# Bias by distance of four heads in one matmul of four rows, the rows repeated by the DMA that writes them

## The chip, the cores and the metric

One core of a Trainium2 chip runs the whole program. The metric is device time in microseconds (us), the median of several executions. The core has TensorE (matmuls, PE in the profile; PEld are its weight loads), VectorE (DVE), ScalarE (ACT), GpSimd (POOL) and SyncE (SP), which here issues nearly all DMA transfers, and sixteen DMA engines that carry them out.

## The reference

A decode step of a hybrid layer. One branch is a gated linear recurrence; the other, where the change lies, is attention in a sliding window with a dilation: three groups of four heads, window 128, 512 or 2048, dilation 1, 4 or 16. A score gets a bias that depends only on the head and on the distance of key and query:

```
def slot_bias(rel_bias, g):
    dist = jnp.arange(N_SLOTS, dtype=jnp.int32) * DILATIONS[g]
    return rel_bias[t5_bucket(dist), g * HEADS_PER_GROUP:(g + 1) * HEADS_PER_GROUP].astype(jnp.float32)
...
    dist = qi + BLK - ki
    in_band = (dist >= 0) & (dist <= N_BACK)
...
    b = jnp.transpose(bias[jnp.clip(dist, 0, N_BACK)], (2, 0, 1))
    s = jnp.einsum('brnqhe,brnkhe->brnhqk', qc, kb, preferred_element_type=jnp.float32)
    s = s * ATTN_SCALE + b
```

## The kernel before

The order of all instructions is written out by hand, and each engine takes its own in that order. The first thousand microseconds are a loop over `units` (index `i`): twelve heads in the order of groups 2, 1, 0, and for each head 16 blocks of 128 tokens and a unit for the 64 sample tokens, so 17 units (`ph = i % 17`) to a head. A unit makes q, k and v of its block (`stage_a`, 24 matmuls z<-w,RH or z<-w,RL on L336, about 5 us), normalizes and transposes them (trc, L376), makes scores S and adds the bias tile T3 (L401, L407), takes the exponential, and multiplies with v; stages of up to four units are interleaved.

The bias of a head is a table of 383 values, one for each distance and BIG where the window ends. `bias_0` loads a 33 x 383 onehot matrix `oh` (L281) and spreads the head's column of `reln` over 128 columns (`lb`, L283). `bias_a` multiplies the two (L290), so that 128 equal rows of 383 come out, copies them to `es_` (L292) and writes them to device memory, to `Dsc[hd]` (L293). `bias_b` reads them back with a row step of 382 in place of 383 (L298, L299), which shifts each row by one against the row ahead of it: that is `T3`, the bias of a block of queries against a block of keys. `bias_0` of the next head `nh` stands at unit 7 of a head, `bias_a` at unit 9, `bias_b` at unit 12. For the first head all stand at the start.

At the start and again while the last head of group 2 and of group 1 runs (`i // 17` 3 and 7), the units also bring in the input x: `x_load` (xt, 512 KB, L224, two buffers), `x_mul` on VectorE (L240, two halves), `x_tr` (transposes trx and the split into RH and RL). At the start `x_norm` takes the squares on ScalarE first (L229). A tile loaded in one unit is used in the next. Other transfers of these stretches are kv outputs (L371), attention outputs Osc (L435), weights wr (L307) and copies from cache to cache out_kv_s (L109), all issued by SyncE in one sequence; an issue waits until what it reads is made and its buffer is free.

Of the kernel before, what the change touches and what calls it, by code (L numbers as in the profile page):

```python
# [11 lines left out]
F32 = mybir.dt.float32  # L12
# [11 lines left out]
HD = 128  # L24
# [6 lines left out]
NBX = 383  # L31
# [11 lines left out]
def program(tc, I, O, C, upto=99, debug=False):  # L43
    nc = tc.nc
    es = ExitStack()
    G = K()
# [4 lines left out]
    PE, ACT, DVE, POOL = nc.tensor, nc.scalar, nc.vector, nc.gpsimd  # L51
    dma = nc.sync.dma_start
# [6 lines left out]
    Dsc = sd("Dsc", [12, 128, NBX])  # L59
# [18 lines left out]
    def pool(stack, name, **kw):  # L78
        return stack.enter_context(tc.tile_pool(name=name, bufs=1, reuse_waits="tile", **kw))
# [5 lines left out]
    ps = es.enter_context(tc.tile_pool(name="ps", bufs=2, space=PSUM))  # L85
# [108 lines left out]
    ap_ = pool(at, "ap")  # L194
    xs_ = ExitStack()
    reln = ap_.tile([33, 12], F32, name="reln")
# [78 lines left out]
    heads = [(g, h) for g in (2, 1, 0) for h in range(4)]  # L275
    Wt, Wr, Tt = {}, {}, {}

    def bias_0(g, h):
        hd = g * 4 + h
        oh = ap_.tile([128, NBX], F32, name="oh", tag="wraw", bufs=4)  # L280
        dma(oh[0:33, :], C["onehot"][:, g, :])  # L281
        lb = ap_.tile([128, HD], F32, name="lb", tag="kqs", bufs=1)
        POOL.tensor_copy(lb[0:33, :], reln[:, hd:hd + 1].to_broadcast([33, 128]))  # L283
        G.ohlb = oh, lb

    def bias_a(g, h):
        hd = g * 4 + h
        oh, lb = G.ohlb
        eb = ps.tile([128, NBX], F32, name="eb", tag="op")
        PE.matmul(eb, lb[0:33, :], oh[0:33, :], start=True, stop=True)  # L290
        es_ = ap_.tile([128, NBX], F32, name="es_", tag="wraw", bufs=4)
        ACT.copy(es_, eb)  # L292
        dma(Dsc[hd], es_)  # L293

    def bias_b(g, h):
        hd = g * 4 + h
# [13 lines left out]
    def w_conv_h(hd_, k):  # L310
        w = ap_.tile([128, 2, 384], F32R, name="w", tag="w", bufs=10)
        ACT.copy(w[:, 0, :], Wr[hd_, k])
        Wt[hd_, k] = w
# [5 lines left out]
    def w_conv(hd_, k, eng):  # L319
        wr = Wr.pop((hd_, k))  # L320
        w = ap_.tile([128, 2, 384], F32R, name="w", tag="w", bufs=10)
        split(w[:, 0, :], w[:, 1, :], wr, eng)
        Wt[hd_, k] = w
# [14 lines left out]
    def stage_b1(u):  # L338
        m, z = u.m, u.z
        if u.stacked:  # L340
            DVE.tensor_add(z[0:NS], z[0:NS], u.zl[0:NS])
        u.ss = ap_.tile([128, 2], F32, name="ss", tag="ss", bufs=3)
        jk = ap_.tile([128, HD], mybir.dt.bfloat16, name="jk", tag="jk", bufs=1)
        for i in range(2):
            ACT.activation(jk[0:m, :], z[0:m, i * 128:(i + 1) * 128], AF.Square, accum_out=u.ss[0:m, i:i + 1])  # L345
        u.rs = ap_.tile([128, 2], F32, name="rs", tag="rs", bufs=3)
        POOL.tensor_scalar(u.ss[0:m, :], u.ss[0:m, :], 1.0 / HD, EPS, ALU.mult, ALU.add)  # L347
        POOL.tensor_tensor(u.rs[0:m, :], u.ss[0:m, :], neghalf[0:m, :], ALU.pow)  # L348

    def stage_b2h(u):  # L350
        m, z = u.m, u.z
        u.vt = ap_.tile([128, 2, HD], F32R, name="vt", tag="vt", bufs=4)
        return u.vt[0:m, 0, :], z[0:m, 256:384]
# [19 lines left out]
    def stage_c(u):  # L373
        m = u.m
        tr = ps.tile([128, 2, 128], F32, name="trc", tag="tr")
        PE.transpose(tr[:, 0, 0:m], u.kvo[0:m, 0, :], ident[0:m, 0:m])  # L376
        PE.transpose(tr[:, 1, 0:m], u.qn[0:m, :], ident[0:m, 0:m])
        if u.smp:
            u.kq = ap_.tile([128, 2, NS], F32, name="kqs", tag="kqs", bufs=1)
            ACT.copy(u.kq, tr[:, :, 0:m])  # L380
        else:
            split(KQ[:, u.slot, :, 0, :], KQ[:, u.slot, :, 1, :], tr, DVE)
# [116 lines left out]
    x_mul(1, D // 2, D)  # L499
    POOL.tensor_scalar(gq, gq, -SCALE, 0.0, ALU.mult, ALU.add)  # L500
    POOL.tensor_scalar(reln[0:32, :], reln[0:32, :], -1.0, 0.0, ALU.mult, ALU.add)
    bias_0(*heads[0])
    w_conv(heads[0], 6, DVE)
    w_conv(heads[0], 7, DVE)
    N = len(units)
# [2 lines left out]
    kqs = []  # L508
# [27 lines left out]
    for i in range(N + 3):  # L536
        u, u1, u2, u3 = get(i), get(i - 1), get(i - 2), get(i - 3)
        nh = heads[i // 17 + 1] if i // 17 + 1 < len(heads) and u is not None else None
        ph = i % 17
        G.i = i  # L540
        late = u1 and u1.stacked
        if late:
            u1.zl = ap_.tile([128, 384], F32, name="zl", tag="wraw", bufs=4)
            ACT.copy(u1.zl[0:NS], u1.z[NS:2 * NS])
        elif u1:
            stage_b1(u1)
        if u2:
            stage_c(u2)
        if u1 and not late:
            ACT.copy(*stage_b2h(u1))  # L550
        if u3:
            stage_e(u3)
        if late:
            stage_b1(u1)
            ACT.copy(*stage_b2h(u1))
        if u:
            stage_a(u, 0)
        elif upto > 1:
            gb_z(i - N, "S" if i == N + 2 else "z", hi=8)
        if nh and ph == 16:  # L560
            w_conv(nh, 4, POOL)
            w_conv_h(nh, 2)
            w_conv_h(nh, 3)
        if u1:
            stage_b2(u1)
        if u and ph == 0 and i:
            for k in (6, 7):
                w_conv_h((u.g, u.h), k)
            w_conv_l((u.g, u.h), 6, DVE)
            w_conv_l((u.g, u.h), 7, POOL)  # L570
        if u1:
            stage_b3(u1)
        if u2:
            stage_d(u2)
        if 0 < ph < 16:
            kgo(2 if i < 136 else 1 + (i % 2 == 0))
        if nh and ph == 16:
            for k in (2, 3):
                w_conv_l(nh, k, DVE)
                w_load(nh, k + 4)  # L580
        if u:
            if 0 < i < 16:
                x_mul(i + 1, D // 2, D)
                x_tr(i + 1, 0)
                if i < 15:
                    x_norm(i + 2)
            if i > 50 and i // 17 in (3, 7) and ph:
                x_mul(ph - 1, D // 2, D)
                x_tr(ph - 1, 0)
            stage_a(u, 1)  # L590
        elif upto > 1:
            gb_z(i - N, lo=8, hi=16)
        if nh and ph == 16:
            w_conv(nh, 5, DVE)
        kgo(2 if u3 and u3.smp or u2 and u2.smp else ph != 16)
        if u3:
            stage_f(u3)
            stage_g(u3)
        if u:
            if 0 < i < 16:  # L600
                x_tr(i + 1, 1)
                x_load(i + 3)
            if i == 17:
                x_scales()
                G.again, G.xg = True, 1
                x_load(0)
                x_load(1)
            if i > 50 and i // 17 in (3, 7) and ph:
                x_tr(ph - 1, 1)
                x_load(ph + 1)  # L610
            stage_a(u, 2)
            if i == 0:
                x_tr(1, 0)
                x_norm(2)
                x_tr(1, 1)
                x_load(3)
        elif upto > 1:
            gb_z(i - N, lo=16)
        if u:
            if i < 15:  # L620
                x_mul(i + 2, 0, D // 2)
            if i > 50 and i // 17 in (3, 7) and ph < 16:
                x_mul(ph, 0, D // 2)
            if i == 0:
                bias_a(*heads[0])
                bias_b(*heads[0])
        if nh:
            if ph == 7:
                bias_0(*nh)
            if ph == 9:  # L630
                bias_a(*nh)
            if ph == 12:
                bias_b(*nh)
            if ph == 11:
                for k in range(4):
                    w_load(nh, k)
            if ph == 13:
                w_conv(nh, 0, POOL)
                w_conv(nh, 1, DVE)
                w_load(nh, 4)  # L640
                w_load(nh, 5)
        if i > 17 and i % 2:
            copy()
        if i == 115:
            k_flush()
            G.xg = 0
            x_open()
        if u1 and u1.smp and u1.h == 3 and u1.g != 0 and upto > 1:
            xs_.close()
            G.kp = pool(kps, "kp", side="right")  # L650
            q = kmake(G.kp, u1.g, (0, 3, 4)[u1.g])
            q.at = i + 2
            q.init()
            q.queries()
            kqs.append(q)
        if i == N - 4:
            k_flush()
            xss_.close()
            gw = pool(gws, "gw", side="right")
            for k in range(4):  # L660
                gb_load(k)
        if N - 4 < i < N:
            for k in range(3):
                if wbr:
                    n = min(wbr)
                    gb_conv(n)
                    if n < 4:
                        gb_load(n + 4)
# [918 lines left out]
```

## Time and profile before

| | |
|---|---|
| median of 3 runs | 2606.82 us (2605.22 to 2612.3) |
| profiled execution | 2603.89 us, its span 2602.1 us |
| PE busy | 2512.8 us, 97% |
| DVE, ACT, POOL busy | 1553.9, 1080.6 and 553.3 us |
| granted TensorE clock, mean | 0.988 |
| transfers of SyncE's queue | 356.31 MB, 44.4% of the sixteen engines' span |

The span runs from the first to the last instruction of the profiled execution; its times, and those of the rows below, count from there. A granted clock of 1.00 is 2.4 GHz.

### The profile page before, as it was taken

To read this page: it belongs to the slowest core of one execution; us is meant where nothing else is said; L and a number is where in the kernel's file an instruction comes from. 1 tells how busy PE (TensorE), PEld (TensorE's weight loads), DVE (VectorE), ACT (ScalarE), POOL (GpSimd) and SP (SyncE) were. 2 spreads that over 40 slices of the span, in tenths; PEclk is the share of its full clock that TensorE was granted. 3 is DMA by queue.
4 is the path that set the end of the run, shared out by engine and by line. 5 is a ranking of instruction groups with operands and counts; after the bars stand their busy time and mean duration, and the time that the engine had idled before them with its cause. 6 is when DMAs were issued, how large, how long until landed. Compare 5 with 4: busy or idle time off the path is not lost. (4 is left out here: it accounts for less than half of the span.)

```text
span 2602.1 us, 44722 instructions
## 1 busy us (share of the span) xinstructions
PE 2512.8 (97%) x15196; PEld 2351.1 (90%) x15196; DVE 1553.9 (60%) x4805; ACT 1080.6 (42%) x3327; POOL 553.3 (21%) x897
## 2 busy tenths in 40 slices
PE   8999999999999999999999998999998999999999
PEld 7999999999999999999988887888887999998988
DVE  6744686777776777557555666655775723432322
ACT  5534453443453443444455545544556621211110
POOL 4422322221221221223223333320000002200000
PEclk9999999999999999999999999999999999999999
DMA  5443564555554343247533333346555569633332
GB/s 150 108 136 95 145 180 138 163 154 151 154 149 118 105 120 111 78 131 235 182 111 134 105 107 117 105 140 197 186 174 171 169 181 345 206 120 116 118 117 68
DMA packets 311289, 376.73 MB, mean 145 GB/s; under 512 B 54915, under 2 KB 254927, under 8 KB 308221
## 3 DMA queue, kind: packets, MB, share of 16 engines
q1 hardware_dynamic: 297028, 356.31, 44.4%
q0 software_dynamic: 14032, 17.57, 2.5%
q8 instruction: 120, 1.97, 0.3%
q14 instruction: 109, 0.89, 0.1%
HBM read 293.55 MB, written 168.31 MB: 177 GB/s over the span
## 5 line engine op out<-in xcount | busy, mean ns | idle before, releaser
L336 PE MATMUL z<-w,RH 128*128 128x384 f32 (+1 forms) x3088 | 889.2, 349 | 4.9 <-POOL w L317 2.4
L760 PE MATMUL zt<-RH,wz 128*128 128x384 f32 (+2 forms) x2560 | 705.9, 359 | 10.5 <-ACT gt L993 9.7
L336 PEld LDWEIGHTS z<-w,RH 128*128 128x128 f32 (+1 forms) x3088 | 553.3, 188 | 14.7 <-POOL w L317 6.5
L760 PEld LDWEIGHTS zt<-RH,wz 128*128 128x128 f32 x2560 | 471.2, 192 | 57.2 <-ACT gt L993 11.0
L336 PE MATMUL z<-w,RL 128*128 128x384 f32 x1544 | 520.3, 337 | 0.1
L760 PE MATMUL zt<-RL,wz 128*128 128x384 f32 (+2 forms) x1280 | 456.8, 357 | 0.0
L336 PEld LDWEIGHTS z<-w,RL 128*128 128x128 f32 x1544 | 291.5, 189 | 0.7 <-DVE RL L94 0.5
L178 DVE CUSTOM_DVE_ANT_0 kjk<-kt,qs 128x128 bf16<-128x128 f32 x768 | 228.1, 297 | 67.5 <-DMA SA<-Dsc 20.4
L760 PEld LDWEIGHTS zt<-RL,wz 128*128 128x128 f32 x1280 | 244.7, 191 | 23.0
L408 ACT ACTIVATE P<-P,o 128x128 f32<-128x128 f32 (+1 forms) x192 | 88.9, 463 | 311.1 <-DVE o L407 311.1
L345 ACT ACTIVATE jk<-z 128x128 bf16<-128x128 f32 (+1 forms) x408 | 113.0, 277 | 237.0 <-PE trc L376 173.6
L94 DVE TENSOR_TENSOR KQ<-trc,KQ 128x256 fp32r<-128x256 f32 x192 | 81.4, 424 | 208.7 <-ACT KQ L93 208.7
L347 POOL TENSOR_SCALAR ss<-ss 128x2 f32<-128x2 f32 (+1 forms) x204 | 44.5, 218 | 714.2 <-ACT jk L345 679.4
L1465 PEld LDWEIGHTS zt<-y1t,w_wlo 128*128 128x128 f32 x1536 | 190.3, 191 | 0.6
L1465 PE MATMUL zt<-y1t,w_wlo 128*128 128x256 f32 (+1 forms) x1536 | 190.6, 286 | 0.0
L1497 PE MATMUL zt<-w_wo,mt 128*128 128x512 f32 x672 | 162.0, 395 | 0.0
L1497 PEld LDWEIGHTS zt<-w_wo,mt 128*128 128x128 f32 x672 | 126.0, 188 | 30.7
L348 POOL TENSOR_TENSOR rs<-ss,neghalf 128x2 f32<-128x2 f32 (+1 forms) x204 | 142.6, 699 | 17.0
L1150 ACT ACTIVATE v<-v,P 128x128 f32<-128x128 f32 x256 | 81.1, 391 | 76.4 <-DMA v<-in_cache_kv_w 60.7
L434 DVE TENSOR_REDUCE o<-op 128x128 f32<-128x256 f32 x192 | 80.6, 420 | 44.9 <-PE op L429 44.8
L1499 DVE TENSOR_TENSOR xr<-zt,xr 128x512 f32<-128x512 f32 (+1 forms) x34 | 23.5, 692 | 137.3 <-PE zt L1497 132.6
L93 ACT CAST mt<-g 128x256 fp32r<-128x256 f32 x72 | 27.1, 388 | 187.2 <-DVE g L1468 172.1
(292 smaller groups left out, 4273.3 us busy)
## 6 DMA issues: line engine op xcount, KB each, us to landing
out_kv_s<-in_cache_kv_w SPq DMA_DIRECT2D x176, 480.0 KB
xt<-in_x_prompt SPq DMA_DIRECT2D x48, 512.0 KB
wr<-in_w_in SPq DMA_DIRECT2D x96, 192.0 KB
kt<-in_cache_kv_w SPq DMA_DIRECT2D x128, 128.0 KB
wzr<-in_w_in SPq DMA_DIRECT2D x32, 512.0 KB
v<-in_cache_kv_w SPq DMA_DIRECT2D x128, 128.0 KB
Osc<-o SPq DMA_DIRECT2D x192, 65.0 KB
ot<-Osc SPq DMA_DIRECT2D x32, 390.0 KB
```

The source lines that it names most:

```text
L94: eng.tensor_sub(l, src, h.bitcast(F32))
L178: DVE.tensor_tensor_reduce(jk, kts[q.tile][:, c], qts[t][:, c], 1.0, 0.0, ALU.mult, ALU.add, q.SC[:, o:o + 1])
L336: PE.matmul(u.z[0:m, :], (RH, RL, RH)[p][:, k, u.cols], Wt[(u.g, u.h), k][:, (0, 0, 1)[p], :], start=(i == 0), stop=(i == 23))
L345: ACT.activation(jk[0:m, :], z[0:m, i * 128:(i + 1) * 128], AF.Square, accum_out=u.ss[0:m, i:i + 1])
L347: POOL.tensor_scalar(u.ss[0:m, :], u.ss[0:m, :], 1.0 / HD, EPS, ALU.mult, ALU.add)
L348: POOL.tensor_tensor(u.rs[0:m, :], u.ss[0:m, :], neghalf[0:m, :], ALU.pow)
L408: ACT.activation(u.P[:, 0:n], u.P[:, 0:n], AF.Exp, bias=u.o[:, 128:129], scale=-1.0, accum_out=u.o[:, 129:130])
L434: DVE.tensor_reduce(u.o[:, 0:128], u.op.rearrange("p a b -> p b a"), AX.X, ALU.add)
L760: PE.matmul(z[:, 0:n], w[:, (0, 1, 0)[p], k, :], (RH, RH, RL)[p][:, k, c0:c0 + n], start=(i == 0), stop=(i == 23))
L1150: ACT.activation(v2s[n][:, h], v2s[n][:, h], AF.Copy, scale=P2[:, h, n:n + 1])
L1465: PE.matmul(z[:, 0:n], wl[k][:, (0, 1, 0)[p], f, :], y1s[c * 8 + k][:, (0, 0, 1)[p], 0:n], start=(i == 0), stop=(i == 23))
L1497: PE.matmul(z[0:m, :], ms_[k][:, (0, 0, 384)[p] + o:(0, 0, 384)[p] + o + m], wo[k][:, (0, 1, 0)[p], e * 4:(e + 1) * 4, :].rearrange("p k c ...
```

## The change

One matmul makes the bias tables of a group's four heads: its weights are the four columns of `reln` as they stand, so that 4 rows of 383 come out, on partitions 0 to 3. The copy takes these four rows, and four DMAs write them to `Dsc`, each reading one partition of `es_` 128 times. `bias_0` and `bias_a` run only ahead of a group's first head; `lb` is gone. `bias_b` is as it was.

```
-    def bias_0(g, h):
-        hd = g * 4 + h
-        oh = ap_.tile([128, NBX], F32, name="oh", tag="wraw", bufs=4)
-        dma(oh[0:33, :], C["onehot"][:, g, :])
-        lb = ap_.tile([128, HD], F32, name="lb", tag="kqs", bufs=1)
-        POOL.tensor_copy(lb[0:33, :], reln[:, hd:hd + 1].to_broadcast([33, 128]))
-        G.ohlb = oh, lb
-
-    def bias_a(g, h):
-        hd = g * 4 + h
-        oh, lb = G.ohlb
-        eb = ps.tile([128, NBX], F32, name="eb", tag="op")
-        PE.matmul(eb, lb[0:33, :], oh[0:33, :], start=True, stop=True)
+    def bias_0(g):
+        G.oh = ap_.tile([128, NBX], F32, name="oh", tag="wraw", bufs=4)
+        dma(G.oh[0:33, :], C["onehot"][:, g, :])
+
+    def bias_a(g):
+
+        eb = ps.tile([4, NBX], F32, name="eb", tag="op")
+        PE.matmul(eb, reln[:, g * 4:g * 4 + 4], G.oh[0:33, :], start=True, stop=True)
         es_ = ap_.tile([128, NBX], F32, name="es_", tag="wraw", bufs=4)
-        ACT.copy(es_, eb)
-        dma(Dsc[hd], es_)
+        ACT.copy(es_[0:4, :], eb)
+        for h in range(4):
+            dma(Dsc[g * 4 + h:g * 4 + h + 1], es_[h:h + 1].unsqueeze(1).to_broadcast([1, 128, NBX]))
...
-                bias_a(*heads[0])
+                bias_a(heads[0][0])
                 bias_b(*heads[0])
         if nh:
-            if ph == 7:
-                bias_0(*nh)
-            if ph == 9:
-                bias_a(*nh)
+            if ph == 7 and nh[1] == 0:
+                bias_0(nh[0])
+            if ph == 9 and nh[1] == 0:
+                bias_a(nh[0])
             if ph == 12:
                 bias_b(*nh)
```

SyncE at the start, before: the issues from the onehot load to the second x tile behind the bias, with the semaphores that each waits for (DMAHW ones count finished transfers, the others instructions of an engine).

```order
L281 DMA oh<-c_onehot 33x383 [waits DMAHW7_49,DMAHW2_49,DVE_49]
L224 DMA xt<-in_x_prompt 128x1024 [waits DMAHW0_49,DVE_49,PE_49]
L293 DMA Dsc<-es__238 128x383 [waits DMAHW1_49,Activation_49]
L298 DMA T_241<-Dsc 128x256 [waits DMAHW1_49]
L299 DMA T_241<-Dsc 128x128 [waits DMAHW3_49]
L371 DMA out_kv_p<-kvo 128x2x128 [waits DMAHW4_49,DVE_49,Pool_49]
L224 DMA xt<-in_x_prompt 128x1024 [waits DMAHW5_49,DVE_49,PE_49]
```

And the same place of the change; the T loads, the kv output and the next x tile stand behind four writes, and the first T load waits for the semaphore of the first write, DMAHW1.

```order
L280 DMA oh<-c_onehot 33x383 [waits DMAHW7_49,DMAHW2_49,DVE_49]
L224 DMA xt<-in_x_prompt 128x1024 [waits DMAHW0_49,DVE_49,PE_49]
L289 DMA Dsc_57<-es__236 128x1x383 [waits DMAHW1_49,Activation_49]
L289 DMA Dsc_57<-es__236 128x1x383
L289 DMA Dsc_57<-es__236 128x1x383 [waits DMAHW3_49]
L289 DMA Dsc_57<-es__236 128x1x383 [waits DMAHW4_49]
L294 DMA T3_242<-Dsc_57 128x256 [waits DMAHW5_49,DMAHW1_49]
L295 DMA T3_242<-Dsc_57 128x128 [waits DMAHW6_49]
L367 DMA out_kv2_p<-kvo_267 128x2x128 [waits DMAHW7_49,DVE_49,Pool_49]
L224 DMA xt_299<-in_x_prompt 128x1024 [waits DMAHW0_49,DVE_49,PE_49]
```

SyncE at unit 9 of the last head of group 2, where the first bias of group 1 is made, in the change; before, one Dsc write stood where four stand, and the rows behind it were the same.

```order
L224 DMA xt<-in_x_prompt 128x1024 [waits DMAHW1_49,PE_49]
L289 DMA Dsc<-es__4705 128x1x383 [waits DMAHW2_49,Activation_49]
L289 DMA Dsc<-es__4705 128x1x383 [waits DMAHW3_49]
L289 DMA Dsc<-es__4705 128x1x383 [waits DMAHW4_49]
L289 DMA Dsc<-es__4705 128x1x383 [waits DMAHW5_49]
L367 DMA out_kv_p<-kvo 128x2x128 [waits DMAHW6_49,DVE_49,Pool_49]
L431 DMA Osc<-o 128x130 [waits DMAHW7_49,DVE_49]
L224 DMA xt<-in_x_prompt 128x1024 [waits DMAHW0_49,PE_49]
```

TensorE at unit 9 ahead of the last head, before.

```order
L336 MATMUL z<-w,RH 128x384 x2
L336 MATMUL z<-w,RL 128x384
L336 MATMUL z<-w,RH 128x384
L290 MATMUL eb<-oh,lb 128x383
L376 MATMUL trc<-ident,kvo 128x128
L377 MATMUL trc<-ident,qn 128x128
```

The same place of the change; the bias product is gone, as at eight more places, and the transpose follows the last z matmul.

```order
L332 MATMUL z<-w,RH 128x384 x2
L332 MATMUL z<-w,RL 128x384
L332 MATMUL z<-w,RH 128x384
L372 MATMUL trc<-ident,kvo 128x128
L373 MATMUL trc<-ident,qn 128x128
```

## Rows read from the trace of the kernel before

**Rows 1.** Windows: stretch, length, busy us of PE, PEld, DVE, ACT, POOL, clock, DMA share, GB/s.

```profile
0.00:1020.00 1020.00, 999.03 (x6281) 963.56 (x6282) 703.86 (x2659) 459.03 (x1849) 264.31 (x547) 1.00 0.48 136
```

**Rows 2.** The bias product's line: count, duration ns min/median/max, first and last start.

```profile
L290 PE MATMUL eb<-oh,lb x24: 482/534/586, 18.9 to 1008.1; 33*128 33x383 f32 x24
```

**Rows 3.** Timeline of PE without and with a bias: start, duration, engine, line, operation.

```profile
1001.93 0.34 PE L336 MATMUL z<-w,RH 128*128 128x384 f32 x1
1002.11 0.27 PE L376 MATMUL trc<-ident,kvo 128*128 128x128 f32 x1
...
1007.37 0.34 PE L336 MATMUL z<-w,RH 128*128 128x384 f32 x1
...
1008.48 0.33 PE L376 MATMUL trc<-ident,kvo 128*128 128x128 f32 x1
```

**Rows 4.** Timeline of SyncE's issues (SPq) at the first place.

```profile
21.10 0.33 SPq L293 DMA_DIRECT2D Dsc<-es__238  x1
23.43 0.32 SPq L298 DMA_DIRECT2D T<-Dsc  x1
...
25.03 0.33 SPq L224 DMA_DIRECT2D xt<-in_x_prompt  x1
```

**Rows 5.** Windows at the first place.

```profile
19.00:22.00 3.00, 2.96 (x13) 2.08 (x13) 1.96 (x3) 2.87 (x10) 0.91 (x3) 1.00 0.61 168
22.00:23.00 1.00, 0.81 (x6) 0.84 (x7) 0.33 (x3) 0.15 (x1) 0.92 (x3) 1.00 0.58 215
```

**Rows 6.** Timeline, first readers of T and of that x tile.

```profile
28.55 0.28 DVE L401 TENSOR_TENSOR P<-S,T 128x128 f32<-128x128 f32 x1
...
30.06 1.06 ACT L229 ACTIVATE XS<-xt 128x1024 fp32r<-128x1024 f32 x1
```

**Rows 7.** Timeline at the second place: the write, the next x load, its reader.

```profile
347.51 0.32 SPq L293 DMA_DIRECT2D Dsc<-es__4733  x1
...
352.88 0.95 SPq L224 DMA_DIRECT2D xt<-in_x_prompt  x1
...
358.93 0.74 DVE L240 SCALAR_TENSOR_TENSOR xt<-xt,xrs,gn 128x512 f32<-128x512 f32 x1
```

**Rows 8.** Windows at the second place.

```profile
345.50:349.00 3.50, 3.50 (x19) 2.71 (x18) 1.91 (x6) 1.91 (x9) 0.68 (x2) 1.00 0.62 162
349.00:350.00 1.00, 1.00 (x10) 1.00 (x9) 1.00 (x5) 0.00 (x0) 0.66 (x2) 1.00 0.66 250
```

**Rows 9.** Timeline at the third place.

```profile
726.82 0.32 SPq L293 DMA_DIRECT2D Dsc<-es__10112  x1
...
732.37 0.37 SPq L224 DMA_DIRECT2D xt<-in_x_prompt  x1
...
738.75 0.74 DVE L240 SCALAR_TENSOR_TENSOR xt<-xt,xrs,gn 128x512 f32<-128x512 f32 x1
```

**Rows 10.** Windows at the third place.

```profile
724.50:728.00 3.50, 3.50 (x20) 2.71 (x19) 1.60 (x3) 2.16 (x9) 0.37 (x2) 1.00 0.61 160
728.00:729.00 1.00, 1.00 (x9) 1.00 (x8) 0.99 (x5) 0.16 (x1) 0.52 (x1) 1.00 0.61 228
```

**Rows 11.** Window of the start.

```profile
4.00:5.00 1.00, 0.00 (x0) 0.00 (x0) 0.00 (x0) 0.00 (x0) 0.00 (x0) 1.00 1.04 414
```

**Rows 12.** Timeline of the start; in brackets the idle time before and what ended it.

```profile
1.20 0.41 SPq L212 DMA_DIRECT2D gn<-in_g_norm  x1
1.65 0.96 SPq L307 DMA_DIRECT2D wr<-in_w_in  x2
...
7.13 1.15 ACT L93 CAST w<-wr 128x384 fp32r<-128x384 f32 x2 [0.86 <-DMA wr<-in_w_in]
```

**Rows 13.** Windows around a pause of TensorE, a later stage.

```profile
1732.00:1736.00 4.00, 0.00 (x0) 0.00 (x0) 3.39 (x7) 0.00 (x0) 2.19 (x4) 0.75 0.27 98
1736.00:1740.00 4.00, 3.87 (x10) 3.09 (x11) 0.68 (x1) 0.58 (x1) 0.54 (x2) 0.50 0.80 233
1740.00:1742.00 2.00, 2.00 (x8) 1.59 (x8) 0.00 (x0) 0.48 (x2) 0.00 (x0) 0.80 1.03 374
```

**Rows 14.** Window of loads to 64 partitions, a later stage.

```profile
1949.50:1953.00 3.50, 3.50 (x17) 2.88 (x16) 0.00 (x0) 2.05 (x6) 0.00 (x0) 1.00 0.50 176
```

More of the change, by code (lines that the diff above doesn't have):

```diff
@@ L501, in program @@
     POOL.tensor_scalar(reln[0:32, :], reln[0:32, :], -1.0, 0.0, ALU.mult, ALU.add)
-    bias_0(*heads[0])
+    bias_0(heads[0][0])
     w_conv(heads[0], 6, DVE)
```

## The prediction

> **What bounds the kernel now.** The change touches only the first part, the units of four head groups that fill the first thousand microseconds. The view to read first is the busy time of that stretch by engine [rows 1]: TensorE works 999 of 1020 us, at a granted clock of 1.00, its full 2.4 GHz; VectorE has 704, ScalarE 459, GpSimd 264, and the transfer engines are busy 48% of the time. So a TensorE instruction that disappears here gives back its time, and work taken from another engine gives nothing until something late stops TensorE. Second comes the bias's own group [rows 2]: twelve products in two passes each, 534 ns a pass. Third are the three places at which a head group's first bias is made, with SyncE's issues, the bytes moved and the first reader of each transfer [rows 4 to 10].
>
> **What goes away.** Nine of the twelve products. A pass's duration overlaps its neighbours, so the price is taken between starts. From the last z matmul of a unit to the transpose that follows it is 0.18 us where no bias stands between (1001.93 to 1002.11), and 1.11 us where one does (1007.37 to 1008.48) [rows 3]. That is 0.93 us each; the distance is the same to 0.02 us at all eleven places inside the pipeline, so 9 x 0.93 = **-8.4 us**. The other three keep their 383 columns and only load 4 weight columns in place of 128: I give them nothing (at most 0.3 us each, the start of the product after its neighbour in the same rows). Nine evictions on ScalarE, twelve copies on GpSimd and nine loads of the onehot matrix on SyncE go too. TensorE idles 21 us of the 1020 for all causes together [rows 1], so these lie under its work and are priced at nothing; should TensorE once wait for such an engine, the price would be negative, a further gain.
>
> **What is added: nothing in number, something in kind.** Dsc is written twelve times as before, 128 rows of 1532 B (196 KB) each. Before, the source was 128 partitions of es_; now it is one partition, read 128 times, and the four writes of a group are issued together, with all later transfers of SyncE behind them. In SyncE's order four Dsc writes stand where one stood at 21 us, 347 us and 727 us; the nine other writes are gone from their places.
>
> The cost of such a write, W, is not in the trace: no row reads one partition with all sixteen transfer engines. Bound below: the spread write. At the first place the xt load ahead (524 KB) accounts for 19.0 to 22.1 us (168 GB/s to 22.0, then 20 KB), and the write for 22.1 to 23.0 us [rows 5], so W is at least 0.9 us. Bound above: one transfer engine's rate. The best stretch without traffic between two places in device memory, 4 to 5 us, moves 414 GB/s with all sixteen engines busy [rows 11], which is 25.9 GB/s for one engine, or for each eight of the 128 partitions that the loads fill; no row shows more for so few. 196 KB at 25.9 GB/s is 7.6 us. A harsher row, loads of 64 partitions at 176 GB/s [rows 14], would make it 196 / 11 = 17.8 us, but these are paced by SyncE's issues (transfer share 0.50). I take **W = 7.6 us**, because one partition is far nearer to eight than to 128, and this row prices eight; I keep 0.9 and 17.8 as ends.
>
> The Trainium skill (SBUF — State Buffer, Door 1: The DMA port swizzle) speaks against this change: partitions 0 to 3 sit on one of sixteen ports, and a transfer over these four is given as 27.6 GB/s. By that W would be 7.1 us and the time 2666 us; no run here shows it yet.
>
> **Where the writes are waited for.** SyncE's transfers go out in the order of issue: the wr loads issued from 1.65 us reached ScalarE only at 7.13 us, behind the xt and gn loads issued before them [rows 12]. So what stands behind the four writes moves 4W = 30.3 us later than the first of them could start. After the last byte it takes 0.4 us more until a reader goes (the write of 22.1 to 23.0 us released the T load at 23.43 us) [rows 4, 5].
> - *First place.* The writes end at 22.1 + 30.3 = 52.4 us. T's two loads wait on SyncE for the first write alone, then queue behind the other three: 196 KB at 414 GB/s, then 0.4 us, is 53.3 us; VectorE reads T at 28.55 us today [rows 6]: 24.8 us late. The xt load behind it (851 KB in all, 2.1 us) lands at 54.9 us; ScalarE's square of it stands at 30.06 us: also 24.8 us, at the same time. VectorE takes instructions in order, and the next transposes of TensorE need its x_mul.
> - *Second place.* The xt load in flight and an Osc store (591 KB) end at 349.1 us (162 GB/s to 349.0) [rows 8]; the writes end at 379.4 us. Behind them stand a kv store, an Osc store and the xt load issued at 352.88 us: 722 KB, 1.7 us, then 0.4: 381.5 us. VectorE's x_mul of that tile stands at 358.93 us [rows 7]: 22.6 us late.
> - *Third place.* By the same count 728.1 us [rows 10] + 30.3 + 1.4 + 0.4 = 760.2 us against the x_mul at 738.75 us [rows 9]: 21.5 us.
>
> Together **+68.9 us** (12W - 22.0 as long as all three stalls are positive). TensorE's buffers hide a part of a stall under one unit, which I do not subtract, since VectorE, the late engine, is itself 70% busy and does not catch up much.
>
> After a pause of that length the clock is low: before 1736 us TensorE does nothing for about 4 us, then works at a granted clock of 0.50, its lower level of 1.2 GHz, to about 1740.8 us (0.80 over 1740 to 1742) [rows 13]. 4.7 us at half speed lose 2.3 us; three times, **+7.0 us**.
>
> **The sum.** 2603.9 (the profiled execution, 1.8 us more than its span, and 2.9 us under the median of the runs) - 8.4 + 68.9 + 7.0 = **2671 us**.
>
> **The rivals.**
> *A, the writes are as quick as before* (W near 0.9): the four end at 25.7 and 352.7 us, before anything waits. Then only the matmuls count: 2595.5 us. For it speaks that the gn load reads one row of device memory 128 times and moves at the 414 GB/s above [rows 11, 12]; against it, that this source was device memory, not one partition. 0.12.
> *B, a partial limit.* At W = 2.5 us the stalls are 8 us, without a fall of the clock, and cancel the saving: 2603.5 us. This is the point from which the sign turns. 0.06.
> *C, one partition is slower than an engine*: W = 17.8 us gives 2603.9 - 1.4 + 191.6 = 2794 us. 0.08.
> *D, the writes are slow but other transfers pass them*: only T waits, issued at 22.1 + 7.6 + 0.4 = 30.1 us; with today's 5.1 us from issue to reader at most, it stalls 4 to 7 us at the first place, none at the others, where T is issued three units of some 5 us behind the writes. 2600 us. The order of arrival at the start speaks against it, though it was seen among spread loads only. 0.09.
> The forecast itself has 0.65.
>
> **Range and chances.** About 0.3% (8 us) is what a measurement here can tell from no change. With W from 6 to 9.5 us the forecast's own range is 2653 to 2695 us. A, B and D hold 0.27 on the other side, so the range goes from A's end, 2596, to 2696 us, and leaves out C and the longest W. Slower: forecast, C and a little of B, 0.75. A lies on the border of 0.3%, half to each side, D and most of B within: same 0.18, faster 0.07.
>
> **What would show it.** TensorE's bias group: six passes, not 24, and 0.18 us at the nine places. VectorE's addition of T waits some 25 us near 28 us; x_mul waits for xt 22 us near 359 and 739 us; in each gap some 30 us of a transfer rate near 26 GB/s, and a granted clock of 0.50 behind it. T's first load is issued near 30 us, which gives W directly. The forecast is wrong if the rate in the gaps stays at hundreds of GB/s (A), or if xt loads land within the writes (D), or if stalls are there, but longer in proportion to W (C).

## The result and the profile after

| | before | after |
|---|---|---|
| median, 4 runs each in turn on one chip | 2608.6 us (2605.22 to 2612.3) | 2671.59 us (2669.45 to 2673.08) |
| ratio, 95% interval | | 1.0248 (1.0235 to 1.0261) |
| span of the profiled execution | 2602.1 us | 2668.9 us |
| PE busy | 2512.8 us, 97% | 2508.4 us, 94% |
| granted clock, mean | 0.988 | 0.976 |

The change makes the kernel slower by 2.5%, some 65 us by the ratio (the two medians of the table lie 63 us apart; a fourth run of before moved its median from 2606.82 to 2608.6 us). TensorE's busy time is almost the same: it works less, and for a while at half its clock. The time went into waiting. The first part, whose first 1020 us before hold 21 us of idle TensorE [rows 1], takes some 64 us longer, and the same columns read over 1085 us show 87 us idle:

```profile
0.00:1085.00 1085.00, 998.08 (x6268) 969.34 (x6269) 703.19 (x2660) 457.33 (x1845) 261.24 (x536) 0.97 0.50 127
```

The bias product's line of after, beside [rows 2]: six passes, at three places.

```profile
L285 PE MATMUL eb<-oh,reln x6: 482/482/482, 21.5 to 771.3; 33*4 33x383 f32 x6
```

SyncE's issues at the first place, beside [rows 4]. The second column is how long the issue itself took; x4 adds four of them.

```profile
23.28 13.46 SPq L289 DMA_DIRECT2D Dsc<-es__236  x4
36.84 7.13 SPq L294 DMA_DIRECT2D T<-Dsc  x1
44.01 7.19 SPq L295 DMA_DIRECT2D T<-Dsc  x1
51.31 0.39 SPq L367 DMA_DIRECT2D out_kv_p<-kvo  x1
51.81 0.40 SPq L224 DMA_DIRECT2D xt<-in_x_prompt  x1
```

The issues of [rows 4] took 0.32 or 0.33 us. Now SyncE stands 7.13 and 7.19 us in two issues that are not writes: while the writes are under way it gets one issue through per write. So a write takes W = 7.2 us, 196 KB at 27.2 GB/s. The packets in the trace agree: the 512 row reads of a burst start over 29.0, 28.6 and 28.8 us at the three places, a quarter of which is 7.1 to 7.3 us. The windows of that place, beside [rows 5], show the same rate from the other side.

```profile
28.00:32.00 4.00, 4.00 (x28) 3.92 (x26) 2.44 (x6) 1.17 (x6) 1.31 (x3) 1.00 0.89 28
32.00:36.00 4.00, 0.27 (x2) 0.00 (x0) 0.00 (x0) 0.00 (x0) 0.00 (x0) 0.89 0.88 27
36.00:50.00 14.00, 0.00 (x0) 0.00 (x0) 0.00 (x0) 0.00 (x0) 0.00 (x0) 0.50 0.87 27
50.00:52.00 2.00, 0.00 (x0) 0.00 (x0) 0.00 (x0) 0.00 (x0) 0.00 (x0) 0.50 0.89 34
52.00:54.00 2.00, 0.00 (x0) 0.00 (x0) 0.00 (x0) 0.00 (x0) 0.00 (x0) 0.50 0.78 128
54.00:56.00 2.00, 0.00 (x0) 0.00 (x0) 0.86 (x4) 0.24 (x1) 0.00 (x0) 0.50 0.96 349
56.00:62.00 6.00, 5.46 (x20) 5.40 (x21) 3.73 (x9) 3.68 (x13) 1.88 (x5) 0.50 0.33 98
62.00:64.00 2.00, 2.00 (x15) 2.00 (x14) 0.70 (x5) 0.00 (x0) 0.21 (x1) 0.90 0.23 66
```

Read the last three columns: for over 20 us the transfer engines are nearly 90% busy and move 27 or 28 GB/s, where [rows 5] show 168 and 215 GB/s. TensorE runs dry at about 32 us, and every engine stands until 54 us. The granted clock is 0.50 for most of the pause and for some 6 us of work behind it.

The second place shows it again, and so does the third (the last line here: 29 GB/s, no instruction on any engine).

```profile
376.00:388.00 12.00, 10.26 (x68) 9.87 (x67) 6.96 (x17) 5.46 (x22) 2.24 (x5) 1.00 0.89 29
388.00:400.00 12.00, 0.00 (x0) 0.00 (x0) 0.00 (x0) 0.00 (x0) 0.00 (x0) 0.59 0.86 27
...
402.00:404.00 2.00, 0.00 (x0) 0.00 (x0) 0.00 (x0) 0.00 (x0) 0.00 (x0) 0.50 0.67 134
404.00:412.00 8.00, 2.99 (x12) 2.99 (x13) 3.73 (x11) 0.96 (x3) 0.46 (x1) 0.50 1.00 303
...
788.00:800.00 12.00, 0.00 (x0) 0.00 (x0) 0.00 (x0) 0.00 (x0) 0.00 (x0) 0.56 0.88 29
```

VectorE's first instruction behind each pause, in brackets its idle time and what ended it; they answer to [rows 6, 7, 9].

```profile
55.10 0.29 DVE L397 TENSOR_TENSOR P<-S,T 128x128 f32<-128x128 f32 x1 [24.27 <-DMA T<-Dsc]
...
407.87 0.75 DVE L240 SCALAR_TENSOR_TENSOR xt<-xt,xrs,gn 128x512 f32<-128x512 f32 x1 [23.56 <-DMA xt<-in_x_prompt]
...
805.81 0.75 DVE L240 SCALAR_TENSOR_TENSOR xt<-xt,xrs,gn 128x512 f32<-128x512 f32 x1 [21.43 <-DMA xt<-in_x_prompt]
```

To add up the difference I set the start of VectorE's qn, the normalized q (L360), of each of the 204 units against the same instruction before (L364). The distance grows by 2.2 us before the first write, by 27.0 us at the first place, 25.6 at the second and 22.0 at the third, each with the units of low clock behind it, and it shrinks by 12.8 us at all other units together: 2.2 + 74.6 - 12.8 = 64.0, against 63.9 read at the last unit. Behind the units 2.9 us more are lost, which makes the 66.8 us between the spans. The profiles of all nine experiments lose 0.8 to 7.9 us there against the same execution of before, so these 2.9 us are no sign of the change.

### The profile page after: what moved, and what is told of

It is laid out like the page before. It is cut to its first block, busy times and chain, and to the rows that moved or that the text cites. A ratio compares the mean times of both kernels' runs of the same rounds, so it can differ in the third digit from the quotient of the medians.

```text
span 2668.9 us, 44633 instructions
## 1 busy us (share of the span) xinstructions
PE 2508.4 (94%) x15178; PEld 2352.6 (88%) x15178; DVE 1553.6 (58%) x4805; ACT 1077.5 (40%) x3318; POOL 549.5 (21%) x885
## 5 line engine op out<-in xcount | busy, mean ns | idle before, releaser
L332 PEld LDWEIGHTS z<-w,RH 128*128 128x128 f32 (+1 forms) x3088 | 556.4, 189 | 13.3 <-POOL w L313 5.5
L756 PEld LDWEIGHTS zt<-RH,wz 128*128 128x128 f32 x2560 | 468.6, 191 | 62.8 <-ACT gt L989 17.8
L756 PEld LDWEIGHTS zt<-RL,wz 128*128 128x128 f32 x1280 | 243.6, 190 | 22.6
L240 DVE SCALAR_TENSOR_TENSOR xt<-xt,xrs,gn 128x512 f32<-128x512 f32 (+1 forms) x98 | 75.6, 773 | 53.2 <-DMA xt<-in_x_prompt 45.9
L93 ACT CAST mt<-g 128x256 fp32r<-128x256 f32 x72 | 27.2, 388 | 190.9 <-DVE g L1464 175.7
```

The source lines that it names most:

```text
L332: PE.matmul(u.z[0:m, :], (RH, RL, RH)[p][:, k, u.cols], Wt[(u.g, u.h), k][:, (0, 0, 1)[p], :], start=(i == 0), stop=(i == 23))
L756: PE.matmul(z[:, 0:n], w[:, (0, 1, 0)[p], k, :], (RH, RH, RL)[p][:, k, c0:c0 + n], start=(i == 0), stop=(i == 23))
```

## The experiments

Two theories stood at the start. **The narrow source**: a write whose source lies on few partitions is slow, and what SyncE issues behind it waits. **The burst**: four writes one behind the other, or the repetition in the source, are what costs, wherever the rows lie. Later runs ask which resource is narrow, whether the queue matters, and what the saving is worth. The medians of before beside these runs were 2606.55 to 2606.57 us.

**1. The same burst from 128 partitions.** One product a group as in the change, but the first head's column spread over 128 weight columns, and four writes of 128 rows each.

```
+        POOL.tensor_copy(G.lb[0:33, :], reln[:, g * 4:g * 4 + 1].to_broadcast([33, 128]))
...
-            dma(Dsc[g * 4 + h:g * 4 + h + 1], es_[h:h + 1].unsqueeze(1).to_broadcast([1, 128, NBX]))
+            dma(Dsc[g * 4 + h], es_)
```

> One product per group as in the change, but its weights are the column of the group's first head repeated 128 times, and all four writes of the group read the 128 rows of es_, one partition for each row, in the same place and order as in the change. So the other three heads of a group get the first head's bias table. Narrow source (the prediction): the writes are quick again (about 0.9 us each), the three stalls go; unit by unit they measure 27, 25.5 and 22 us in the change, so 2671.6 - 74.5 = about 2597 us. Rival, the burst of four writes ahead of the x tiles is what costs, whatever it reads: 2671 us. Rival, half and half: 2620 to 2650 us.

Measured: 2595.16 us (6 runs), ratio 0.9959 (0.9944 to 0.9973). SyncE issues all four in 1.79 us and T's first load at 24.03 us:

```profile
21.46 1.79 SPq L290 DMA_DIRECT2D Dsc<-es__238  x4
24.03 0.32 SPq L295 DMA_DIRECT2D T<-Dsc  x1
```

There is no pause at any of the three places. Four writes together cost nothing here, so the burst as such is out.

**2 and 3. Four partitions for each head, as neighbours or apart.** Sixteen weight columns, four equal ones to a head; each of a head's four rows is read 32 times. In the one kernel the rows of head h lie on partitions 4h to 4h+3, in the other on h, 4+h, 8+h and 12+h. Everything else is the same in both. As neighbours:

```
+        POOL.tensor_copy(G.lb[0:33, 0:16].rearrange("k (h j) -> k h j", h=4), reln[:, g * 4:g * 4 + 4].unsqueeze(2).to_broadcast([33, 4, 4]))
...
+            dma(Dsc[g * 4 + h].rearrange("(j r) c -> j r c", j=4), es_[h * 4:h * 4 + 4].unsqueeze(1).to_broadcast([4, 32, NBX]))
```

and apart:

```
+        POOL.tensor_copy(G.lb[0:33, 0:16].rearrange("k (j h) -> k j h", h=4), reln[:, g * 4:g * 4 + 4].unsqueeze(1).to_broadcast([33, 4, 4]))
...
+            dma(Dsc[g * 4 + h].rearrange("(j r) c -> j r c", j=4), es_[h:16:4].unsqueeze(1).to_broadcast([4, 32, NBX]))
```

> Each head's row is made on four neighbouring partitions (4h to 4h+3), and its write reads these four, 32 times each. If a single partition is what is narrow, four give four times the 27 GB/s seen in the change: a write of 1.8 us, and about 2597 to 2600 us. If what is narrow is shared by neighbouring partitions, 7.2 us a write as in the change, and 2665 to 2675 us. If any source that is read repeatedly is slow: also about 2671 us. The Trainium skill (SBUF — State Buffer, Door 1: The DMA port swizzle) puts four neighbours that begin at a multiple of four on one port, and so stands with the second.

> As the run with four neighbours, but a head's four partitions are h, 4+h, 8+h and 12+h; the writes are alike in count, size and repeats. If neighbours share what is narrow, and partitions four apart do not: 1.8 us a write and about 2597 to 2600 us, while the run with neighbours stays at 2665 to 2675 us. If eight in a row share it: two of these at once, 3.6 us a write, 14.4 us for four in place of 28.8 us, and about 2615 to 2630 us. If a single partition is narrow: as the run with neighbours, both about 2600 us. If any repeated source is slow: both about 2671 us.

Measured: neighbours 2652.21 us (4 runs), ratio 1.017 (1.0147 to 1.0192); apart 2603.47 us (10 runs), ratio 0.9987 (0.9976 to 0.9997). The window of 24 to 28 us, and SyncE's four issues, of the neighbours:

```profile
24.00:28.00 4.00, 3.65 (x24) 3.35 (x25) 2.50 (x6) 2.22 (x5) 1.86 (x4) 1.00 0.21 25
...
22.91 9.06 SPq L290 DMA_DIRECT2D Dsc<-es__238  x4
```

The same of the partitions apart:

```profile
24.00:28.00 4.00, 3.67 (x24) 3.35 (x24) 2.99 (x6) 2.88 (x10) 1.07 (x4) 1.00 0.31 100
...
21.89 3.87 SPq L290 DMA_DIRECT2D Dsc<-es__238  x4
```

A transfer share near 0.25 is about four engines of sixteen. These few engines move 25 GB/s from four neighbouring partitions and 100 GB/s from four that lie four apart. So neither an engine's own speed nor one partition's is the limit (four neighbours are not faster than one partition, 27.2 GB/s), but something that four neighbouring partitions share. The Trainium skill's map (SBUF — State Buffer, Door 1: The DMA port swizzle) has partitions 0 to 3 on one port, at 27.6 GB/s, and 0 to 15 on four, at 104 GB/s; the measured 25 to 27.2 and 100 GB/s agree. The 100 GB/s of the rows apart can as well be the own rate of about four engines (25.9 GB/s each by [rows 11]); these runs do not separate the two. With the rows apart, a stall of 6 us is left at the first place (T lands with VectorE idle 3.8 us before it) and 2 us at the second. Why the neighbours stall only 16 and 17 us at the second and third place, with 23 us at the first, is not settled; free engines may let part of the x tile pass, which no run tests.

**4 and 9. Thirty-two partitions for each head.** Every head's column stands 32 times among 128 weight columns, each write reads 32 partitions four times. This computes all that the change computes.

```
+        POOL.tensor_copy(G.lb[0:33, :].rearrange("k (h j) -> k h j", h=4), reln[:, g * 4:g * 4 + 4].unsqueeze(2).to_broadcast([33, 4, 32]))
...
+            dma(Dsc[g * 4 + h].rearrange("(j r) c -> j r c", j=32), es_[h * 32:h * 32 + 32].unsqueeze(1).to_broadcast([32, 4, NBX]))
```

> One product makes all four heads as in the change, but each head's column is repeated 32 times among the 128 weight columns (one more copy on GpSimd per group), so that a head's table stands on 32 partitions, and each write reads these, 4 times each. The full result is computed. Narrow source: 32 partitions are wide enough, a write takes about 1 us, no stall is left, about 2597 us, under the kernel before by the nine matmul pairs: 2608.6 - 8.4 to 12. Any repeated source is slow: about 2671 us. The burst is what costs: about 2671 us.

Measured: 2595.88 us (4 runs), ratio 0.9957 (0.9939 to 0.9974). The writes and the next loads at the first place:

```profile
21.36 2.63 SPq L290 DMA_DIRECT2D Dsc<-es__238  x4
24.53 0.34 SPq L295 DMA_DIRECT2D T<-Dsc  x1
```

No stall is left (the unit that lost 25 us in the change loses 0.5 us), so reading a row several times costs no time as long as the rows lie wide enough. The transfers themselves are not quite as quick: from 23 to 26 us they run at 213 to 257 GB/s, where experiment 1, with 128 partitions, has 302 to 366 GB/s from 22 to 24 us. The second measurement, for the size of the gain:

> The kernel with each head's table on 32 rows once more, with more runs, to size what the change saves where nothing stalls. If the price of the nine products is the distance between starts alone, 9 x 0.93 = 8.4 us: 2598 us, ratio 0.9968. If the unit loop's end is the measure (12.7 us earlier in the first profile): 2594 us, ratio 0.9951.

Measured: 2598.39 us (5 runs), ratio 0.9963 (0.9949 to 0.9976), 9.6 us (6.3 to 13.3) faster than before. In the unit loop the first profile of this kernel gains 13.0 us, the second 10.0, counted from the first unit on: two executions of one kernel differ by 3 us there, and the times alone do not decide between 8.4 and 12.7 us. The units do: the nine that lost a product, each with the unit behind it, give 8.9 us in the first profile and 8.5 in the second. The rest are steps at other units, and the largest that recurs (0.9 us in both, at the third unit of the sixth head) stands in the profile of experiment 6 as well, which keeps all twelve products. So at least part of these steps belongs to the one profiled execution of before, and not to the saving.

**5. Fewer rows.** The change with only two of a group's four tables in full.

```
-        for h in range(4):
-            dma(Dsc[g * 4 + h:g * 4 + h + 1], es_[h:h + 1].unsqueeze(1).to_broadcast([1, 128, NBX]))
+        for h, n in enumerate((128, 128, 16, 16)):
+            dma(Dsc[g * 4 + h:g * 4 + h + 1, 0:n], es_[h:h + 1].unsqueeze(1).to_broadcast([1, n, NBX]))
...
-        hd = g * 4 + h
+        hd = g * 4 + h % 2
```

> As the change, but of a group's four tables only the first two are written in full (128 reads of one partition each); of the other two 16 rows are written, and the third and fourth head add the tables of the first and second. Left out: the right bias of six heads. If the stall follows the bytes that leave one partition at a time (7.2 us for 196 KB), a group's writes take 2.25 x 7.2 = 16.2 us in place of 28.8, each of the three stalls is 12.6 us shorter, 37.8 us together, and the time is 2671.6 - 37.8 = 2634 us, with stalls near 13, 11 and 9 us. If each issue of such a write costs its time whatever its rows, four issues stand there as in the change: 2671 us. If the buffers ahead of TensorE take up part of a shorter stall: below 2625 us.

Measured: 2632.31 us (4 runs), ratio 1.0102 (1.0085 to 1.0118). The stalls by the unit's starts are 12.3, 10.4 and 8.0 us, and each is 12.9 to 13.1 us shorter than in the change; 12.6 was expected of 1.75 writes fewer. The stall follows what is read from the narrow source, not the number of writes.

**6. The narrow write alone.** The kernel before, all twelve products at their places, with the source of each write narrowed.

```
-        dma(Dsc[hd], es_)
+        dma(Dsc[hd:hd + 1], es_[0:1].unsqueeze(1).to_broadcast([1, 128, NBX]))
```

> The kernel before with one edit: each of the twelve writes reads one partition of es_ 128 times in place of 128 partitions; nothing is grouped, the products and the places stay. If what costs is that four slow writes stand together and the next loads behind them, one write of 7.2 us is hidden at all places but the first, where T waits for it: T's load is issued 6.3 us later, so some 6 to 8 us, 2613 to 2615 us, with SyncE held at the next issue for about 7 us at every place. If a narrow write costs its time wherever it stands, 12 x 6.3 = 76 us: 2682 us. If it is hidden at the first place as well: 2607 us.

Measured: 2616.85 us (5 runs), ratio 1.0044 (1.0031 to 1.0058): 10.3 us, not 76, and not 0. The write and the next issue at the first place, and ScalarE's reader of an x tile at unit 11 of the first head:

```profile
21.45 0.62 SPq L293 DMA_DIRECT2D Dsc<-es__238  x1
30.31 0.34 SPq L298 DMA_DIRECT2D T<-Dsc  x1
...
93.40 1.06 ACT L229 ACTIVATE XS<-xt 128x1024 fp32r<-128x1024 f32 x1 [2.92 <-DMA xt<-in_x_prompt]
```

The first place loses 5.4 us. Beyond what I expected, x tiles that are loaded behind the write are late too: 3.0 us at unit 11 of the first head and 1.8 us where the first write of group 1 stands. The third place, and the other places, where no x comes in, move by about 1 us or less. So a lone write of 7.2 us is mostly hidden, and the loss of the change needs four together. SyncE does not stand 7 us in an issue here. T's load at the first place is issued late because it waits for its own write, and then takes 0.34 us; where the first write of group 1 stands, the kv issue behind it takes 0.39 us and the Osc issue after that 1.68 us. So a few transfers fit behind one slow write.

**7. Another queue.** The four writes of a group on GpSimd's queue.

```
-            dma(Dsc[g * 4 + h:g * 4 + h + 1], es_[h:h + 1].unsqueeze(1).to_broadcast([1, 128, NBX]))
+            nc.gpsimd.dma_start(Dsc[g * 4 + h:g * 4 + h + 1], es_[h:h + 1].unsqueeze(1).to_broadcast([1, 128, NBX]))
```

> As the change, but the four writes of a group are issued on GpSimd's queue; all other transfers stay on SyncE's. If the stall comes from SyncE's order (its issues held behind the slow writes, and what it issues later waiting in the same queue), the xt loads pass the writes, only T at the first place waits for the first write and then shares the engines with the other three: a stall of 7 to 14 us there, little at the second and third place, 2603 to 2614 us. If the transfer engines themselves are held by the slow reads, whatever queue these are in, the stalls stay at 20 us or more and the time near 2670 us. If GpSimd is held at its own issues, kvo and the x split wait for it: stalls again, but with GpSimd named as what ended them.

Measured: 2670.11 us (4 runs), ratio 1.0244 (1.0228 to 1.0259): like the change. GpSimd issues the second place's four writes at once, and SyncE, which now has none of them, still stands 12.59 and 10.57 us in two issues (the timelines of both).

```profile
370.10 2.15 POOL L289 DMA_DIRECT2D Dsc<-es__4705  x4 [4.64 <-ACT jk L341]
...
376.60 12.59 SPq L431 DMA_DIRECT2D Osc<-o  x1
389.29 10.57 SPq L224 DMA_DIRECT2D xt<-in_x_prompt  x1
```

The queues' shares of the sixteen engines over 372 to 400 us (packets, MB, share): the writes' queue q0 holds them, SyncE's queue q1 moves 0.11 MB.

```profile
q0 software_dynamic: 244, 0.76, 89.6%
q1 hardware_dynamic: 235, 0.11, 1.4%
```

So SyncE's order is not the cause: whatever queue the slow reads are in, they occupy the sixteen engines that every other transfer needs. The Trainium skill (DMA: Bandwidth & Descriptors, Issuing engines are not separate DMA queues) says that transfers of all issuers run on the same sixteen engines; this run agrees.

**8. The nine products put back.** The kernel of experiment 4 with nine spare products at the old places.

```
+            if ph == 9 and nh[1]:
+                eb = ps.tile([128, NBX], F32, name="eb", tag="op")
+                PE.matmul(eb, gq[0:33, :], RH[0:33, 0, 0:NBX].bitcast(F32), start=True, stop=True)
```

> The kernel with each head's table on 32 rows (2595.9 us), with nine products put back at the places where the kernel before has them: same shape and type (33 rows, 128 columns, 383 columns, two passes), operands that lie there anyway, the result unused; the nine loads, the GpSimd copies and the evictions stay away. If the gain of that kernel is TensorE's time alone, all of it goes: 2606 to 2607 us. By the price between starts, 0.93 us each, 8.4 us go: 2604 us, and the 2 to 4 us that remain are of the loads and evictions. If half of the gain came from these: 2601 us.

Measured: 2604.84 us (11 runs), ratio 0.9999 (0.9991 to 1.0008). Its products take what they took before:

```profile
L631 PE MATMUL eb<-RH,gq x18: 482/534/586, 73.8 to 1006.7; 33*128 33x383 f32 x18
```

The gain is gone, though nine loads, nine evictions and their GpSimd copies stay away: the time is that of before within 0.1%. In the trace, the nine units and those behind them are 0.3 us ahead of before, where they were 8.9 and 8.5 us ahead without the spare products. The gain lies in TensorE's products.

## Why the prediction was right, step by step

**What goes away, -8.4 us: right in kind.** Experiment 8 shows that the products are nearly the whole of it (all but 0.3 us at their units) and that the other work under TensorE gives nothing that the runs resolve. In the trace most units that lost their product start their qn 1.14 us earlier and give back 0.15 us in the next, 0.99 us against the forecast's 0.93; the nine together give 8.8 us. The rest of the 12.8 us of this profile are small steps at units without a bias, which in part belong to the execution of before (experiment 9); measured by times, the saving is 9.6 us (6.3 to 13.3).

**W = 7.6 us: right, a little long.** The issues give 7.2 us. The 25.9 GB/s from the row at full traffic [rows 11] was the right neighbour, and the upper end of 17.8 us fell: [rows 14] were limited by something else. The forecast had two readings for that rate: what one transfer engine moves, and what eight of the 128 partitions give. The first is not what limits the write: in the change nearly all sixteen engines were busy for 27.2 GB/s, and in experiment 2 about four for 25. That the forecast's number held under either reading is luck, since both are a sixteenth of the 414 GB/s. The estimate of 7.1 us from the figure of 27.6 GB/s in the Trainium skill (SBUF — State Buffer, Door 1: The DMA port swizzle) was nearer still.

**Where the writes are waited for: the right three waits, by the right transfers.** T at the first place, x tiles at the other two, as the idle times of VectorE show. The first unit behind each pause starts 25.4, 23.3 and 21.1 us later (69.8 us) against the forecast's 24.8, 22.6 and 21.5 (68.9). This closeness is partly luck. With the measured W the term 12W - 22.0 is 64.4 us. The other 5.4 us are mostly in the transfers behind the writes, which I let run at 414 GB/s at once. The last row reads of the three bursts start at 53.6, 403.0 and 802.6 us, and VectorE goes on 1.5, 4.8 and 3.2 us later, where I counted 0.9, 2.1 and 1.8 us: 4.7 us more. The rows of before already had a slower rate for these transfers, 166 to 170 GB/s in their first 2 us, against 128 GB/s over 52 to 54 us and 134 over 402 to 404 us in the change.

```profile
24.00:26.00 2.00, 1.68 (x12) 1.62 (x12) 1.17 (x3) 1.07 (x3) 0.73 (x2) 1.00 0.60 166
354.00:356.00 2.00, 2.00 (x16) 2.00 (x15) 1.85 (x9) 0.41 (x3) 1.25 (x3) 1.00 0.82 166
733.00:735.00 2.00, 2.00 (x14) 2.00 (x13) 1.76 (x6) 1.04 (x6) 0.88 (x2) 1.00 0.77 170
```

So the 414 GB/s of the start [rows 11] was the wrong row for them; what holds their rate down, before as after, no run here settles.

**T's first load near 30 us: wrong.** It was issued at 36.84 us. I had the issues pass freely and only the data wait; in fact the third and fourth write's issues themselves stood behind the writes ahead. It changed no sum at the first place, since T's data had to wait for the fourth write either way. At the second place the x tile's own issue went through only at 402.6 us, as the writes ended; whether that cost anything is not shown.

**The clock, +7.0 us: right in kind, large by 2 us.** The units that follow lose 1.6, 2.3 and 0.9 us, 4.8 us together, at a granted clock of 0.50 as in [rows 13]. Behind the first pause it lasts some 6 us; behind the second TensorE is busy for only 2.99 of 8 us at that clock (404 to 412 us), so part of the slow time is spent waiting in any case. The division between stall and clock is rough, since the first unit behind a pause already runs at 0.50.

**The rivals.** A (as quick as before) and C (17.8 us) fell by the rate in the gaps. B does not hold for one partition, though experiment 3 shows such a case: 100 GB/s, a stall of 6 us at one place and 2 at another, and a time 3 us from before. D, in which other transfers pass, fell twice, by the waits for x in the change and by experiment 7, where the writes had a queue of their own.

The sum came out 0.6 us under the median because small misses cancel, which is luck. Between the two profiles the first units behind the pauses lose 69.8 us for 68.9, the clock 4.8 for 7.0, and the other units give back 12.8 for 8.4. Not forecast were the 2.9 us behind the units and 2.2 us before the first write, where a weight load reaches ScalarE 1.1 us later and the clock is 0.50 over 18 to 20 us. That start comes and goes among the experiments: 0.3 to 0.8 us in 1, 3, 4, 5, 6, 8 and 9, and 1.8 in 2, again at 0.50. In 7 the clock stays at 1.00, and its 2.2 us have another cause: GpSimd issues the four writes for 2.36 us first, and VectorE waits 2.55 us for what GpSimd computes next.

## What to carry to other kernels

A product with four weight columns takes about the pass of one with 128 (482 ns against 534 in [rows 2] and in experiment 4), so rows that a transfer is to repeat cost nothing extra if the weights are spread: 32 columns to a head kept the gain (ratio 0.9963) that four single rows turned into a loss of 65 us. Price a transfer by how its SBUF rows are spread, not by its bytes alone: 196 KB from one partition took 7.2 us and kept the sixteen engines nearly 90% busy meanwhile. And look at what stands behind it: twelve such writes one by one cost 10 us, the same twelve in three bursts some 75 us.

## What the runs showed of the hardware

- A slow transfer shows in the issuer: SyncE stood 7.13 and 7.19 us in single issues, where those of [rows 4] took 0.32 or 0.33 us, and 12.59 us when the slow transfers were in another queue.
- The transfer engines look busy (0.86 to 0.89) while they move 27 GB/s: the share alone doesn't show throughput.
- Four neighbouring partitions gave 25 GB/s and four partitions four apart 100 GB/s, with about a quarter of the engines busy in both.
